# Twenty gate blocks as ten pairs of seven half-depth products

## The chip, the cores and the metric

The kernel runs on one core of one Trainium2 chip. The metric is the device time in microseconds (us) of one execution on that core. The engines are named as the profile names them: PE (TensorE, matmuls), PEld (its weight loads), DVE (VectorE), ACT (ScalarE), POOL (GpSimd) and SP (SyncE, which here only issues DMAs).

## The reference, cut to what matters

One layer of a backbone, for 2048 sample tokens and 128 prompt tokens. The normalized activations go through one wide input projection, three token mixers work on parts of it, and each branch's result is weighted by a sigmoid gate:

```python
proj = jnp.einsum('btd,de->bte', xn, w_in)            # 2176 tokens x 1024 x 7696
qkv, beta, dec, z_a, u_b, v_b, z_b, x_c, z_c, gates = jnp.split(proj, points, axis=-1)
...
br = jnp.stack([o_a, o_b, o_c], axis=2)               # A: gated delta rule, B: spatial MLP, C: Fourier
pb = jnp.einsum('btnw,nwd->btnd', br, w_branch)
gt = jax.nn.sigmoid(gates.reshape(B, T, N_BRANCH, D_MODEL))
merged = jnp.einsum('btnd,btnd->btd', gt, pb)
return jnp.einsum('btd,de->bte', merged, w_out), s_f, s_b
```

The gates are 3072 of the projection's columns: 24 blocks of 128.

## The kernel before

Channels lie on the 128 partitions and tokens run along the free axis. The 2176 x 1024 activations stand in SBUF all along as two float16 halves, `xh` and `xl` (value and remainder), each 128 x 8 x 2176. A weight block of 128 output channels is 128 x 8 x 128, also in two halves (`whi`, `wlo`). A float32-like product is three float16 matmuls per depth step k: whi.xh, whi.xl, wlo.xh; all of them are issued in line 249 (`mm`), so the trace groups them by tile names, not by line. Tokens go in five groups, `TBS`: four of 512 and one of 128; one group of one block is 24 matmuls into one PSUM bank.

A weight block comes by one 512 KB DMA into `wst`, is squared and summed on ACT (L318), gets a scale that is a power of two (DVE, L277 to L279), and is split: `whi` by ACT (L330), `wlo` by DVE (L331: `wst * s - whi`). `getw(n, ahead)` takes the next of one list, `wlist`, and lets so many be prepared ahead; `weight_step()` does one stage of that.

The stages, in order of PE's time in the profiled execution:

- to 160 us: activations, modulation, the first projections
- 160 to 433: q, k, v, 12 blocks, each followed by a conv of three taps over the 2176 tokens (DVE, ACT, POOL) and one store per block
- 433 to about 1010: 22 gate blocks, `gate_block`: per token group 24 matmuls, a sigmoid on ACT (L1496), a store on SP (L1497). Beside them the delta rule's preparation (`kq`, `qr` loads of L999, the triangular inverses of `base_inverse` as a ping-pong between DVE L1126 and POOL L1127, to 870), then the start of the scan. The list's squares of later weights (`later_squares`, ACT) and the sums for the output gate (`gate_rows`: 16 loads of 256 KB, each with four DVE operations of 256 columns, L489 and L491) go beside the gate blocks as well, one step per token group
- 1010 to 1135: branch B's V from four blocks `v4hi`/`v4lo` used together; then U, Z_B and Z_C to 1345, and the Fourier branch C to about 1700
- 881 to about 1600: `scan()`, 34 steps of a chain PE - DVE - ACT - DVE - PE (the tiles `sk`, `sv`, `v`, `u`, `S`; L1316, L1243, L1244, L1338, L1357), beside all of the above
- 1700 to 1732 the last two gate blocks, then `pace.drain()`, and the merges of branches 1 (to 1832) and 2 (to 1980), each 8 blocks of half depth with a multiply by the stored gate (L1821)
- 1980 to 2247: the merge of branch 0 with the output projection, already in seven half-depth products instead of eight (DVE L2003 and L1938 read their banks in between), and the stores.

The order on each engine is fixed when the program is built: a scheduler simulates the program and writes one list per engine; each engine takes its list in order and waits at each instruction for what it needs. What goes beside the gemms is set by `Pace`: a stage calls `pace.tick(us)` with the PE time it has just issued, and the generator (preparation or scan) is taken one step further per quota: `QUOTA` = 1.6 us of gemm per step of the preparation, `SCAN` = 1.15 us per step of the scan. `tc.high_priority()` puts an instruction ahead of others that are ready.

Of the kernel before, what the change touches and what calls it, by code (L numbers as in the profile page):

```python
# [20 lines left out]
P = 128  # L21
D = 1024
KT = 8
# [9 lines left out]
SCAN = 1.15  # L33
# [5 lines left out]
EARLY = 22  # L39
# [157 lines left out]
def hybrid_flow_kernel(ctx: ExitStack, tc: tile.TileContext, x_prompt, x_sample, state_delta, c, c_ctx, w_ada,  # L197
# [178 lines left out]
    for i, (n_, g) in enumerate(_blocks()):  # L376
        wlist.append((w_blk[i], KT, "z" if n_ == C_ZA else "v" if n_ == C_V else "w", 4))
# [3 lines left out]
    goal = [0]  # L381
    wdone, wnext, wread, wlate, bwp, wsteps = [], [0], [], [0], [], []

    def read_next(p_=None):
        if p_ is not None:
            st = sb(p_, [P, D], "ab", bufs=7).rearrange("p (k c) -> p k c", k=KT)
            load(st, wlist[len(wread)][0].rearrange("p (k c) -> p k c", k=KT))
            wread.append(st)
        elif len(wread) < min(len(wdone) - len(wsteps) + 2, len(wlist)):
            src, nkt, tag, bufs = wlist[len(wread)][0:4]  # L390
            wread.append(read_w(src, nkt))

    def begin():

        i = len(wdone)
        if i >= goal[0] or (wlist[i][2] in "bc" and not bwp):
# [426 lines left out]
    vqs = sb(dp, [P, 12], "vqs")  # L823
# [4 lines left out]
    cfs = ExitStack()  # L828
    cf = sb(pool(cfs, "cfp", 1), [P, 2, _CW - _CF], "cf", F16)
    v4s = ExitStack()  # L830
    v4p = pool(v4s, "v4p", 1)
    v4.extend(sb(v4p, [P, 4, KT, P], n_, F16) for n_ in ("v4hi", "v4lo"))
    a1 = ExitStack()
    a1p = pool(a1, "a1p", 2)
    def decays():
# [24 lines left out]
        dtb = sb(a1p, [P, 2, H], "dtb", bufs=1)  # L860
        al = sb(a1p, [P, 2, H], "al", bufs=1)
# [37 lines left out]
        for d in range(2):  # L899
            pt = bank(ps_d, [HN, P])  # L900
            PE.transpose(pt, flat(gam)[:, d * HN:(d + 1) * HN], ident)
            gr = sb(a1p, [HN, P], "gr", bufs=1)
            V.tensor_copy(gr, pt)
            SY.dma_start(gamR[d], gr)
# [38 lines left out]

    flip = [0]
    pace.start(decays(), 1.2)
    for ct in range(12):
        w = getw(1, 2)
        for half in range(1):
# [12 lines left out]
            y = sb(a1p, [P, LP - 2], "cy")  # L961
            V.tensor_scalar(y, raw[:, 0:LP - 2], convw(0, ct), None, ALU.mult)
            V.scalar_tensor_tensor(y, raw[:, 1:LP - 1], convw(1, ct), y, ALU.mult, ALU.add)
            V.scalar_tensor_tensor(y, raw[:, 2:LP], convw(2, ct), y, ALU.mult, ALU.add)
            for c0 in range(0, LP - 2, CQ):
                c1 = min(c0 + CQ, LP - 2)
                A.activation(raw[:, 1 + c0:1 + c1], y[:, c0:c1], AF.Sigmoid)  # L967
                G.tensor_tensor(y[:, c0:c1], y[:, c0:c1], raw[:, 1 + c0:1 + c1], ALU.mult)  # L968
            G.dma_start(qkvD[ct], y)
            if ct < 4 or ct > 7:  # L970
                A.activation(raw[:, 1:LP - 1], y, AF.Square, accum_out=vqs[:, ct:ct + 1])
    pace.drain()
    a1.close()

# [22 lines left out]
    def rows(part, t):  # L997
        x = sb(d2, [P, H, P], "kq" if part else "qr", bufs=3 if part else 2)
# [20 lines left out]
    def prep(g, ci, t, nxt, held):  # L1019
# [21 lines left out]

        more(1, lambda: rows(1, nxt))
        ps = turned(1)
# [29 lines left out]
        for d in range(2):  # L1073
            n_ = sb(d2, [P, WB], "n32", bufs=3)
# [4 lines left out]
            n16 = sb(d2, [P, 2, WB], "n16", F16, bufs=4)  # L1079
# [10 lines left out]
        for d in range(2):  # L1090
            q_ = sb(d2, [P, WB], "n32", bufs=3)
            V.tensor_mul(q_, ps, dc[:, d, :])
            p16 = sb(d2, [P, 2, WB], "n16", F16, bufs=4)
# [306 lines left out]
    def bounds():  # L1400
# [6 lines left out]
        A.activation(sb(dq, [P, 1024], "E"), s0.rearrange("p d x -> p (d x)"), AF.Square, scale=math.sqrt(8.0), accum_out=vqs[:, 4:5])  # L1407
        V.tensor_reduce(bnds[:, 0:1], vqs[:, 0:4], AX.X, ALU.add)
        qs, iqs = scales(bnds[:, 0:1], dp, "qsc")
        yield 1  # L1410
        V.tensor_reduce(bnds[:, 1:2], vqs[:, 8:12], AX.X, ALU.add)
        V.scalar_tensor_tensor(bnds[:, 1:2], bnds[:, 1:2], 8.0 * NTOK, vqs[:, 4:5], ALU.mult, ALU.add)
# [109 lines left out]
    osums = sb(cp, [P, 16], "osums")  # L1522

    def later_squares():


        for i in range(40):
            st = sb(ep, [P, 4, P], "st", bufs=3)
            n, j = (i // KT, i % KT) if i < 24 else (3, i - 24)
            SY.dma_start(st, w_brb[n, j].rearrange("p (k c) -> p k c", k=4) if n < 3 else  # L1530
                         w_outb[j // 2].rearrange("p (k c) -> p k c", k=KT)[:, j % 2 * 4:j % 2 * 4 + 4])
            yield 1
            A.activation(st, st, AF.Square, accum_out=bsums[:, 3 + i:4 + i] if n < 3 else osums[:, j:j + 1])
            yield 1
        b16 = sb(ep, [P, 40], "b16", BF16, bufs=1)
        V.tensor_copy(b16[:, 0:24], bsums[:, 3:27])
        V.tensor_copy(b16[:, 24:40], osums)
        yield 1
        ps = bank(ps_x, [P, 28])
        mm(ps[:, 0:24], ones16, b16[:, 0:24])  # L1540
        halves = b16[:, 24:40].rearrange("p (a j h) -> p a h j", a=2, h=2)
        for i in range(4):
            mm(ps[:, 24:28], ones16, halves[:, i // 2, i % 2], i == 0, i == 3)
        V.tensor_copy(bsums[:, 3:27], ps[:, 0:24])
        exponents(ps[:, 0:24], bscale)
        exponents(ps[:, 24:28], oscale)

    def one_by_one(*gens):
        for gen in gens:
            yield from gen  # L1550
# [222 lines left out]
    def as_pair(hi, lo, src, s):  # L1773
        made = A.activation(hi, src, AF.Copy, scale=s)  # L1774
        V.scalar_tensor_tensor(lo, src, s, hi, ALU.mult, ALU.subtract)  # L1775
        return made

# [19 lines left out]
    pace.drain()  # L1797
    cs_.close()
# [6 lines left out]
    def merge(n, first, inv, step):  # L1805

        for db in range(KT):
# [3 lines left out]
            for t0, tn in TBS:  # L1811
# [6 lines left out]
                ps = bank(ps_d if swap[0] else ps_mm, [P, tn])  # L1818
# [6 lines left out]
                weight_step()  # L1825
# [6 lines left out]
    late_pool = pool(ctx, "late", 1, side="right")  # L1832
# [5 lines left out]
    merge(1, True, inv1, first_step)  # L1838
    cws.extend(getw(KT, 0))
# [342 lines left out]
```

## Time and profile before

| | |
|---|---|
| median of 3 runs | 2252.34 us (2251.59 to 2254.46) |
| the profiled execution | 2248.82 us, span 2247.0 us |
| mean granted TensorE clock | 0.980 |
| busy: PE, DVE, ACT, POOL | 94%, 59%, 47%, 37% of the span |
| matmuls | 16494 |
| DMA traffic | 418.12 MB, mean 186 GB/s |

Read the table as one core that multiplies nearly all the time. "Busy" counts from an instruction's start to its end on its engine; idle time is what the views of waits name. The span is the time from the first to the last instruction; the execution's own time is 1.8 us longer. Line numbers such as L1496 are those of the kernel before, unless the text says "after".

### The profile page before, as it was taken

To read this page: it belongs to the slowest core of one execution; us is meant where nothing else is said; L and a number is where in the kernel's file an instruction comes from. 1 tells how busy PE (TensorE), PEld (TensorE's weight loads), DVE (VectorE), ACT (ScalarE), POOL (GpSimd) and SP (SyncE) were. 2 spreads that over 40 slices of the span, in tenths; PEclk is the share of its full clock that TensorE was granted. 3 is DMA by queue.
4 is the path that set the end of the run, shared out by engine and by line. 5 is a ranking of instruction groups with operands and counts; after the bars stand their busy time and mean duration, and the time that the engine had idled before them with its cause. 6 is when DMAs were issued, how large, how long until landed. Compare 5 with 4: busy or idle time off the path is not lost. (4 is left out here: it accounts for less than half of the span.)

```text
span 2247.0 us, 43529 instructions
## 1 busy us (share of the span) xinstructions
PE 2106.8 (94%) x16494; PEld 1238.3 (55%) x16494; DVE 1321.2 (59%) x2735; ACT 1045.5 (47%) x2404; POOL 841.1 (37%) x1058
## 2 busy tenths in 40 slices
PE   7989999999999999999999999799999996869997
PEld 3454444455555554555656557587775443435553
DVE  5656844356658653457765566667534567346766
ACT  6655743466655553455434555566535231012222
POOL 0221332234524434222333444355221027456654
PEclk9999999999999999999999999899999998989999
DMA  9855731377777854555555565564305985854541
GB/s 383 287 156 173 263 116 61 113 245 244 252 238 228 266 175 134 183 187 155 155 188 164 182 191 164 161 177 142 107 31 185 299 294 183 284 173 141 172 143 47
DMA packets 269170, 418.12 MB, mean 186 GB/s; under 512 B 43400, under 2 KB 142112, under 8 KB 266656
## 3 DMA queue, kind: packets, MB, share of 16 engines
q1 hardware_dynamic: 218240, 328.94, 46.0%
q10 hardware_dynamic: 39824, 44.05, 5.9%
q0 software_dynamic: 10896, 42.36, 5.1%
q8 instruction: 129, 2.11, 0.4%
q14 instruction: 81, 0.66, 0.1%
HBM read 269.79 MB, written 145.45 MB: 185 GB/s over the span
## 5 line engine op out<-in xcount | busy, mean ns | idle before, releaser
L249 PE MATMUL b<-xh,whi 128*128 128x512 f16 (+1 forms) x1920 | 650.0, 348 | 1.9 <-ACT whi L330 1.8
L249 PE MATMUL b<-xl,whi 128*128 128x512 f16 (+1 forms) x1920 | 651.6, 348 | 0.0
L249 PE MATMUL b<-xh,wlo 128*128 128x512 f16 (+1 forms) x1920 | 649.5, 348 | 0.0
L249 PEld LDWEIGHTS <-whi 128*128 128x128 f16 x4416 | 411.7, 98 | 365.5 <-issue 20.5
L249 PEld LDWEIGHTS <-wlo 128*128 128x128 f16 x2208 | 216.6, 98 | 174.1 <-issue 1.1
L249 PEld LDWEIGHTS <-xh 128*128 128x128 f16 x1512 | 119.2, 98 | 29.9
L1127 POOL TENSOR_TENSOR E<-E,XB 128x31 f32<-128x31 f32 (+15 forms) x155 | 97.4, 628 | 95.3 <-DVE XB L1126 88.0
L1496 ACT ACTIVATE sg<-b,winv 128x512 f32<-128x512 f32 (+1 forms) x120 | 74.0, 621 | 125.3 <-PE b L249 97.5
L968 POOL TENSOR_TENSOR cy<-cy,raw 128x545 f32<-128x545 f32 (+1 forms) x48 | 64.5, 1370 | 181.2 <-ACT raw L967 181.2
L249 PEld LDWEIGHTS <-pa 128*128 128x128 f16 x648 | 63.4, 98 | 93.1 <-ACT pa L1774 18.1
L1823 POOL TENSOR_TENSOR mrow<-mrow,sg 128x512 f32<-128x512 f32 (+1 forms) x40 | 46.8, 1177 | 177.7 <-DMA big<-in_w_outb_dram 140.2
L249 PEld LDWEIGHTS <-bhi 128*128 128x128 f16 x640 | 60.9, 99 | 87.7 <-issue 30.2
L249 PE MATMUL b<-xh,bhi 128*128 128x512 f16 (+1 forms) x320 | 86.5, 362 | 22.4 <-DVE sg L1821 20.8
L249 PE MATMUL b<-o,whi 128*128 128x256 f16 (+1 forms) x576 | 93.9, 268 | 14.2 <-DVE gt L1938 12.2
L249 PE MATMUL b<-wlo,xh 128*128 128x128 f16 x544 | 94.6, 219 | 0.0
L249 PE MATMUL b<-whi,xl 128*128 128x128 f16 x544 | 94.6, 219 | 0.0
L249 PE MATMUL b<-whi,xh 128*128 128x128 f16 x544 | 94.6, 219 | 0.0
L1126 DVE TENSOR_TENSOR XB<-XB,E 128x31 f32<-128x31 f32 (+15 forms) x155 | 52.7, 340 | 64.9 <-POOL E L1127 64.7
L331 DVE SCALAR_TENSOR_TENSOR wlo<-wst,wsc,whi 128x1024 f16<-128x1024 f32 x52 | 68.5, 1319 | 36.7 <-ACT whi L330 36.7
L1202 POOL COPY R<-ES 32x256 f16<-32x256 f16 x136 | 55.7, 409 | 91.7 <-PE b L249 86.7
L249 PE MATMUL b<-big,pa 128*128 128x512 f16 x372 | 86.7, 379 | 3.3 <-DVE st L2003 2.4
L249 PE MATMUL b<-xl,pa 128*128 128x512 f16 x276 | 67.0, 387 | 19.1 <-ACT pa L1774 17.8
(537 smaller groups left out, 4508.6 us busy)
## 6 DMA issues: line engine op xcount, KB each, us to landing
wst<-in_w_blk_dram SPq DMA_DIRECT2D x58, 512.0 KB, 3.5
g<-sg SPq DMA_DIRECT2D x96, 256.0 KB, 3.5
sg<-g SPq DMA_DIRECT2D x64, 256.0 KB, 4.4
qkv<-cy POOLq DMA_DIRECT2D x12, 1089.0 KB, 5.3
dc<-dec SPq DMA_DIRECT2D x17, 512.0 KB, 4.3
kq<-qkv SPq DMA_DIRECT2D x34, 256.0 KB, 4.9
kv<-tok POOLq DMA_DIRECT2D x17, 512.0 KB, 4.8
n<-n ACTq DMA_DIRECT2D x34, 256.0 KB, 5.6
```

The costliest lines, as they stand in the source:

```text
L249: newest[0] = PE.matmul(out, l, r, start=start, stop=stop, skip_group_check=reopened)
L331: w.low = V.scalar_tensor_tensor(w.lo, st, s, w.hi, ALU.mult, ALU.subtract)
L968: G.tensor_tensor(y[:, c0:c1], y[:, c0:c1], raw[:, 1 + c0:1 + c1], ALU.mult)
L1126: V.tensor_tensor(t3, X3[:, 0:k, k:k + 1].to_broadcast([P, k, n_]), E3[:, k:k + 1, k:32].to_broadcast([P, k, n_]), ALU.mult)
L1127: G.tensor_tensor(E3[:, 0:k, k:32], E3[:, 0:k, k:32], t3, ALU.subtract)
L1202: G.tensor_copy(R16[32 * B:32 * B + 32, :, :, B], ES[0:32, :, B, :, wR])
L1496: A.activation(sg, ps, AF.Sigmoid, scale=w.inv)
L1823: G.tensor_tensor(mr, mr, gt, ALU.add)
```

## The change

Twenty of the 22 early gate blocks are done two at a time (`two_gates`). With the depth halved (A11, A12: first 1088 tokens; A21, A22: last 1088 tokens; second index: depth half) and the two blocks' weights halved in depth (B11, B21 of one block, B12, B22 of the other), the 2 x 2 product is made with seven half-depth products in the Strassen-Winograd form instead of eight. Each product is 12 matmuls on 368, 360 or 360 tokens (`THIRDS`). Three PSUM banks, R, Y and X, collect them; Y is read, then added into, then read (t2, t3, t4), X once (t1, b22). Between them DVE reads the partial sum out of the bank (`total`, L1673 after).

- The token sums S1 to S4 (`tsum`, in float16 halves) are made beside q, k, v; S1 takes the place of `x[:, 0:4, 1088:]` in `xh`, `xl` (two DMAs from DRAM) while the pairs run, and the original comes back behind them (two more).
- The weights of a pair (`pair_weights`): seven half-depth pairs hi/lo, three subtractions on POOL, in steps set by the product's number (units 1, 8, 10, 11, 15, 17, 19, 20 of 21).
- `later_squares` goes to q, k, v. `gate_rows` goes from the preparation to the last two of the early gate blocks, three steps per token group, just ahead of V.
- The conv of q, k, v goes in four chunks of 545 columns with four stores per block.
- `SCAN` is 1.35; `pace.drain()` stands behind the first merge, which gets `pace.tick`, one `weight_step` fewer per group, and only the `ps_mm` banks while the scan runs.
- Buffers: `kq` 3 to 2, `n32` 3 to 2, `n16` 4 to 3; the pools of `cf` and `v4` are opened behind the pairs.

```diff
-SCAN = 1.15
+SCAN = 1.35
...
-EARLY = 22
+PAIRS = 10
+EARLY = 2 * PAIRS + 2
+HALF = NTOK // 2
+THIRDS = [(0, 368), (368, 360), (728, 360)]
...
+    def token_sums():
+        for l, x in enumerate((xh, xl)):
+            SY.dma_start(a21D[:, l], x[:, 0:4, HALF:])
+        for k in range(4):
+            for a, b, cn in THIRD:
+                f11, f12, f21, f22 = [sb(ep, [P, cn], "sg", bufs=4) for _ in range(4)]
+                for on, f, kk, ts in ((G, f21, k, b), (V, f11, k, a), (G, f22, k + 4, b), (V, f12, k + 4, a)):
+                    on.tensor_tensor(f, xh[:, kk, ts], xl[:, kk, ts], ALU.add)
+                yield 1
+                V.tensor_tensor(f22, f21, f22, ALU.add)
...
+                st = sb(ep, [P, 2, cn], "st", F16, bufs=3)
+                as_pair(st[:, 0], st[:, 1], f22, 1.0)
+                SY.dma_start(s1D[:, :, k, a], st)
+                yield 1
+                for i, f in enumerate((f11, f21, f12)):
+                    as_pair(tsum[:, i, 0, k, a], tsum[:, i, 1, k, a], f, 1.0)
+                    yield 1
...
+            b11, b21, b12, b22 = [st[:, q] for st in sts for q in (slice(0, 4), slice(4, 8))]
+            w0 = slot()
+            self.b11 = put(w0, 0, b11)
+            G.tensor_tensor(b11, b12, b11, ALU.subtract)
+            G.tensor_tensor(t2, b22, b11, ALU.subtract)
+            G.tensor_tensor(b12, b22, b12, ALU.subtract)
+            self.t2 = put(w0, 4, t2)
+            yield 17
...
     pace.drain()
+    for _ in beside:
+        pass
+    first_pair.upto(20)
     a1.close()
+    for l, x in enumerate((xh, xl)):
+        SY.dma_start(x[:, 0:4, HALF:], s1D[:, l])
...
-    gates_rows = one_by_one(later_squares(), gate_rows())
-    for i in range(EARLY):
-        gate_block(2 if i < EARLY - 3 else 4, 2)
...
+        def total(out, ps, other):
+            with tc.high_priority():
+                V.tensor_tensor(out, ps, other, ALU.add)
...
+            R = bank(ps_mm, [P, cn])
+            multiply(R, w.b11, tokens(0, a))
+            p1 = sb(ep, [P, cn], "sg", bufs=4)
+            with tc.high_priority():
+                A.copy(p1, R)
+            Y = bank(ps_mm, [P, cn])
+            multiply(Y, w.t2, s2)
+            u2 = sb(ep, [P, cn], "st", bufs=3)
+            total(u2, Y, p1)
+            multiply(R, w.b21, tokens(4, a), False)
...
+            multiply(Y, w.t3, s3, False)
+            u3 = sb(ep, [P, cn], "st", bufs=3)
+            total(u3, Y, p1)
+            X = bank(ps_mm, [P, cn])
+            multiply(X, w.t1, tokens(0, b))
+            total(u3, X, u3)
+            put_off(u3, d2, b)
+            multiply(Y, w.t4, tokens(4, b), False)
+            total(p1, Y, p1)
+            put_off(p1, d1, b)
+            multiply(X, w.b22, s4, False)
+            total(u2, X, u2)
+            put_off(u2, d2, a)
...
+    for l, x in enumerate((xh, xl)):
+        SY.dma_start(x[:, 0:4, HALF:], a21D[:, l])
+    sums_.close()
...
+    gates_rows = gate_rows()
+    for i in range(2):
+        gate_block(4 - i, 3)
     for _ in gates_rows:
         pass
```

How the lists of the engines change is shown at three places.

DVE in the middle of the preparation, before: beside the ping-pong of the inverses (`XB`, L1126) stand a weight's scale and its `wlo` of 1024 columns.

```order
L328 TENSOR_TENSOR winv_5086<-wsc_5082,xsc_384 128x1
L1126 TENSOR_TENSOR XB_4257<-XB_4257,E_4258 128x192
L331 SCALAR_TENSOR_TENSOR wlo_5007<-wst_4649,wsc_5082,whi_5006 128x1024
L1045 TENSOR_TENSOR tok_5092<-b_5096,ss_624_5093 128x512
L1126 TENSOR_TENSOR XB_4257<-XB_4257,E_4258 128x175
L1126 TENSOR_TENSOR XB_4257<-XB_4257,E_4258 128x156
```

The same place after (L1258 is the former L1126, L947 the `lo` half of `as_pair`, L1673 `total`, L1208 the preparation's `n`):

```order
L1673 TENSOR_TENSOR st_6436<-b_6323,sg_6321 128x360
L1673 TENSOR_TENSOR st_6436<-b_6438,st_6436 128x360
L947 SCALAR_TENSOR_TENSOR wlo_6398<-wst_5888,wsc_6193,whi_6397 128x512
L947 SCALAR_TENSOR_TENSOR wlo_6337<-wt_781_6086,wsc_6193,whi_6336 128x512
L1258 TENSOR_TENSOR XB_6146<-XB_6146,E_6147 128x135
L947 SCALAR_TENSOR_TENSOR wlo_6398<-wst_5889,wsc_6193,whi_6397 128x512
L1673 TENSOR_TENSOR sg_6321<-b_6323,sg_6321 128x360
L1258 TENSOR_TENSOR XB_6146<-XB_6146,E_6147 128x156
L947 SCALAR_TENSOR_TENSOR wlo_6479<-wst_5888,wsc_6193,whi_6478 128x1024
L1258 TENSOR_TENSOR XB_6146<-XB_6146,E_6147 128x175
L1673 TENSOR_TENSOR st_6351<-b_6438,st_6351 128x360
```

The totals, which PE's next product into the same bank waits for, now stand in one queue with the halves of the next pair's weights and with the inverses.

DVE ahead of V, before: the scan's operations and the last of the four `v4lo` (L331).

```order
L1244 SCALAR_TENSOR_TENSOR S_1424_10892<-S_9595,S_1424_10892 128x512
L1197 SCALAR_TENSOR_TENSOR Q_1245_9345<-b_11320,Q_1245_9345 32x256
L277 TENSOR_SCALAR wsc_11370<-b_11368 128x1
L278 TENSOR_SCALAR wsc_11370<-wsc_11370 128x1
L279 TENSOR_SCALAR wsc_11370<-wsc_11370 128x1
L328 TENSOR_TENSOR winv_11374<-wsc_11370,xsc_384 128x1
L1581 COPY vinv_11455<-winv_11374 128x1
L1316 SCALAR_TENSOR_TENSOR sv_10911<-b_10965,neg_1283,sv_10911 128x128 x4
L331 SCALAR_TENSOR_TENSOR v4lo_1315<-wst_11048,wsc_11370,v4hi_1314 128x1024
```

After, ahead of V (L496 is the former L491 of `gate_rows`, L1376 the former L1244, L1489 the former L1357):

```order
L496 SCALAR_TENSOR_TENSOR st_11091<-st_11174,scT_105,st_11091 128x256 x3
L1470 TENSOR_TENSOR sv_11069<-b_11254,beta_1279 128x512
L496 SCALAR_TENSOR_TENSOR st_11091<-st_11174,scT_105,st_11091 128x256
L1363 SCALAR_TENSOR_TENSOR Q_10452<-b_11532,Q_10452 64x256
L496 SCALAR_TENSOR_TENSOR st_11091<-st_11278,scT_105,st_11091 128x256
L1376 SCALAR_TENSOR_TENSOR u_11268<-sv_11069,u_11268 128x512
L496 SCALAR_TENSOR_TENSOR st_11091<-st_11278,scT_105,st_11091 128x256 x2
L1348 SCALAR_TENSOR_TENSOR R_1349_10442<-b_11577,R_1349_10442 64x4x64
L496 SCALAR_TENSOR_TENSOR st_11091<-st_11278,scT_105,st_11091 128x256
L1489 SCALAR_TENSOR_TENSOR S_10807<-S_10807,egl_1281,b_11336 128x128 x4
```

All 64 operations of `gate_rows` now stand among the scan's steps and the four `v4lo`, and each waits for a load of its own.

SP where the gate blocks begin, before: stores of gates (`g`), a weight, the first loads of the preparation.

```order
L1497 DMA g_3908<-sg_3937 128x512
L1497 DMA g_3908<-sg_3996 128x512
L291 DMA wst_4255<-in_w_blk_dram 128x1024
L1497 DMA g_3908<-sg_4088 128x512
L999 DMA kq_3947<-qkv 128x4x128
```

After:

```order
L294 DMA wst_4175<-in_w_blk_dram 128x1024
L1105 DMA xl_97<-s_1315 128x4x1088
L1105 DMA xh_96<-s_1315 128x4x1088
L294 DMA wst_4554<-in_w_blk_dram 128x1024
L1698 DMA g_4512<-sg_4585 128x368
L294 DMA wst_4555<-in_w_blk_dram 128x1024
L1669 DMA g_4512<-st_4610 128x368
L1131 DMA kq_4528<-qkv 128x4x128
```

The two loads of S1 now stand ahead of the first pair's stores, of the second pair's weights and of the preparation's first loads.

More of the change, by code (lines that the diff above doesn't have):

```diff
@@ L944, in hybrid_flow_kernel @@
+    beside = one_by_one(token_sums(), later_squares())
     flip = [0]
@@ L1548, in one_by_one, with part @@
[L1548 to L1554 removed]
+    def part(ps, w, r, fresh):
+        for k in range(4):
+            mm(ps, w[0][:, k, :], r[0][:, k, :], fresh and k == 0, False, not fresh)
+            mm(ps, w[0][:, k, :], r[1][:, k, :], False, False, not fresh)
+            mm(ps, w[1][:, k, :], r[0][:, k, :], False, k == 3, not fresh)
@@ new lines, in hybrid_flow_kernel, with after @@
+    cur = first_pair
+    for i in range(PAIRS):
+        nxt = pair_weights(i + 1) if i < PAIRS - 1 else None
+        def after(u):
+            if nxt is not None:
+                nxt.upto(u)
+            elif u == 15:
+                wlimit[0] += 2
+                fetch(18)
+            elif u > 15:
+                weight_step()
+        two_gates(i, cur, after)
+        cur = nxt
+    for l, x in enumerate((xh, xl)):
+        SY.dma_start(x[:, 0:4, HALF:], a21D[:, l])
+    sums_.close()
```

211 lines of the change are left out of this document (145 added, 66 removed).

## The prediction

> **What bounds the kernel now.** I read the busy shares of the page and the mean clock first, then the table by stage, then who waits for whom inside the stages that change, then single groups for prices.
>
> ```profile
> PE 2106.8 (94%) x16494; PEld 1238.3 (55%) x16494; DVE 1321.2 (59%) x2735; ACT 1045.5 (47%) x2404; POOL 841.1 (37%) x1058
> core 0: 2247.0 us, clock 0.980
> 160.00:440.00 280.00, 280.00 (x1767) 140.06 (x1764) 154.02 (x174) 140.64 (x203) 75.11 (x97) 1.00 0.41 139
> 440.00:881.00 441.00, 434.21 (x2758) 236.85 (x2756) 267.26 (x676) 245.99 (x685) 180.35 (x266) 1.00 0.71 223
> 881.00:1016.00 135.00, 131.32 (x1178) 77.33 (x1176) 60.05 (x160) 62.18 (x138) 37.72 (x65) 0.99 0.62 193
> 1345.00:1600.00 255.00, 231.19 (x3262) 192.76 (x3260) 168.63 (x423) 159.18 (x473) 114.52 (x157) 0.95 0.52 156
> ```
>
> The columns of the last four rows are window, length, then busy time (instructions) of PE, PEld, DVE, ACT, POOL, the granted clock, the DMA share and GB/s. PE is the bound: 94% of the span, and in the stages that the change touches first (q, k, v and the gate blocks) it multiplies without a gap at full clock. So a matmul column taken out of 440 to 1016 us is time, as long as nothing else becomes late. DVE has 174 us free of 441 there. The Fourier stage is the exception, with 24 us of PE idle and a clock of 0.95.
>
> **The columns.** The last gate block stands alone, so its matmul times are clean: it starts at 1710.07 and its last matmul is followed by the next stage's first at 1732.13.
>
> ```profile
> 1710.07 0.38 PE L249 MATMUL b<-xh,whi 128*128 128x512 f16 x1
> ...
> 1730.79 0.22 PE L249 MATMUL b<-xh,whi 128*128 128x128 f16 x1
> ...
> 1732.13 0.17 PE L249 MATMUL b<-bsc2b,ones 128*128 128x1 bf16 x1
> ```
>
> 96 matmuls of 512 columns take 1730.79 - 1710.07 = 20.72, or 0.2158 us each; 24 of 128 take 1.34, or 0.0558 each. The line through both is 0.4167 ns per column and 2.4 ns per matmul, so 368 columns cost 0.1557 and 360 cost 0.1524 us. A block is 22.06 us, two are 44.12. A pair is 7 products of 12 matmuls for each third: 7 x 12 x (0.1557 + 2 x 0.1524) = 38.68 us. That is 5.44 less per pair, **-54.4 us** for ten. (Twelve matmuls more per pair are counted in it.) Nothing else on PE changes in amount.
>
> **Pairs: the reopened banks.** PE writes Y, DVE adds it into a partial sum, and only then may PE add the next product into Y. There are 3 reopenings per third: T3 and T4 into Y, b22 into X; b21 into R waits likewise for ACT's copy. I count 90 for DVE. Between a bank's last matmul and its reopening lies at least one product of 12 matmuls, 1.83 us. DVE's part:
>
> ```profile
> L2003 DVE TENSOR_TENSOR st<-b,sg x16: 676/681/692, 2003.3 to 2224.6; 128x512 f32<-128x512 f32 x16
> L1938 DVE SCALAR_TENSOR_TENSOR gt<-b,binv,gt x72: 342/475/485, 1917.6 to 2195.8; 128x256 f32<-128x256 f32 x64, 128x128 f32<-128x128 f32 x8
> PE b L249 <- DVE gt L1938: 5.1, 6, 2.2
> PE b L249 <- DVE st L2003: 2.4, 4, 1.5
> 2085.00:2100.00 15.00, 11.70 (x78) 7.44 (x77) 12.55 (x15) 4.67 (x6) 8.23 (x7) 1.00 0.61 211
> ```
>
> Between 0.475 us at 256 and 0.681 at 512 columns, a total of 360 is about 0.56 us, which fits into 1.83 when DVE is free. The output projection at the end is made in the same way and is the nearest measure: 24 reopenings with a slack of 12 x 0.216 = 2.6 us cost 2.4 us of PE waits for L2003 (the first two rows are duration min/median/max; the third and fourth are total us, times, longest). The lower end for ninety is nothing, or -6.8 if even the present idle of that stage went; the upper takes both waits, (2.4 + 5.1)/24 x 90 = 28 us. I take L2003 alone, 0.1 us each: **+9**.
>
> What makes them late is DVE's load in that stage, since the queue is in order:
>
> ```profile
> L331 DVE SCALAR_TENSOR_TENSOR wlo<-wst,wsc,whi x52: 1272/1284/2135, 127.5 to 1660.2; 128x1024 f16<-128x1024 f32 x52
> L1095 DVE SCALAR_TENSOR_TENSOR n<-n,n 128x512 f16<-128x512 f32 x34 | 23.9, 709 | 1.8 <-ACT n L1094 1.6
> L491 DVE SCALAR_TENSOR_TENSOR st<-st,scT,st x56: 466/479/924, 134.7 to 732.6; 128x256 f32<-128x256 f32 x56
> L489 DVE TENSOR_SCALAR st<-st,scT x8: 331/334/351, 134.2 to 715.8; 128x256 f32<-128x256 f32 x8
> L1126 DVE TENSOR_TENSOR XB<-XB,E x155: 177/359/426, 481.3 to 869.8; 128x31 f32<-128x31 f32 x10, 128x60 f32<-128x60 f32 x10, 128x87 f32<-128x87 f32 x10, 128x112 f32<-128x112 f32 x10
> DVE XB L1126 <- POOL E L1127: 64.7, 99, 2.4
> L1823 POOL TENSOR_TENSOR mrow<-mrow,sg 128x512 f32<-128x512 f32 (+1 forms) x40 | 46.8, 1177 | 177.7 <-DMA big<-in_w_outb_dram 140.2
> L1243 ACT ACTIVATE v<-sv 128x512 f16<-128x512 f32 x12 | 7.5, 624 | 3.0 <-DVE sv L1316 3.0
> ```
>
> Added: 150 totals x 0.56 = 84; the `lo` halves, 46 of 512 columns x 0.71 and 10 of 1024 x 1.28, instead of 20 x 1.28, +20. Gone: the part of `gate_rows` that ran there, about 24. So 267 + 84 + 20 - 24 = 347 us of some 440, 79% instead of 61%. The preparation's inverses end at 870, only 11 us ahead of the scan; but they are paced with room, and DVE already waits 64.7 us for POOL in that ping-pong, out of which the added queue can come. POOL gets 27 subtractions at the 1.18 us of L1823, 32 us; ACT gets fewer squares and more copies, about 0.62 us each as in L1243. Both stay below 60%.
>
> [...]
>
> **The swap of S1, the first weights, q, k, v.** Two loads of 1.09 MB go out right behind the last q, k, v matmul and are first needed by T1, the fifth product.
>
> ```profile
> gt<-g SPq DMA_DIRECT2D x8, 1024.0 KB, 5.5
> xt<-in_x_t_dram SPq DMA_DIRECT2D x3, 2048.0 KB, 11.2
> ```
>
> 2.2 MB at 2 MB in 11.2 us land after about 12 us; four products are 4 x 1.868 = 7.5 us, and the preparation's first matmuls can stand between. The bounds are 0 and 4; **+2**. Behind the loads on SP wait the next weights (not needed for 38 us) and the first `kq` (the preparation has its slack). The way back is shorter than one gate block's first two token groups, 8 us of 22; for that and the block's own weight **+1** (0 to 3). In q, k, v, DVE gets 12 units of 10 operations of 360 columns, 67 us, and the first pair's halves, 9: 154 + 76 = 230 of 280. ACT gets 48 copies and 40 squares at L1243's 0.62, 55: 196 of 280. POOL gets 24 sums and 36 more stores; even at 1.18 us for each, 71, it stands at 146. The copies that free PE's banks are put first, so all of it is covered by 280 us of gapless PE; if the cover fails, a late `wlo` costs PE a few us. I take **+1** (0 to 6).
>
> **The start of V.** This is where I expect the largest give-back. `gate_rows`, 56 x 0.479 + 8 x 0.334 = 29.5 us of DVE, lay in the slack of the preparation and now lies in the last two gate blocks, where the scan and the four weights of V (4 x 1.28) want DVE too. Counted over the list with these durations, from the second block's weight to the last `v4lo` DVE has 67 us of work where PE has 61. `gate_rows` works on two free buffers, and each load has to land before two to four of these operations:
>
> ```profile
> st<-in_w_ada_dram SPq DMA_DIRECT2D x16, 256.0 KB, 3.7
> L1316 DVE SCALAR_TENSOR_TENSOR sv<-b,neg,sv 128x128 f32<-128x128 f32 x48 | 13.5, 344 | 2.5 <-PE b L249 2.4
> L1244 DVE SCALAR_TENSOR_TENSOR v<-sv,v 128x512 f16<-128x512 f32 x12 | 11.5, 960 | 1.2 <-ACT v L1243 1.2
> ```
>
> A hop of the scan is 4 x 0.344 + 0.624 (L1243 above) + 0.96 = 3.0 us, and in the new list three of its steps stand there nearly back to back, with 0.5 to 2 us of matmuls between a hop's ends: about 5 us short per step. The two shortages overlap; 67 - 61 = 6 is the least that I see, 6 + 15 = 21 both in full. Bounds 0 (the loads' waits fall into gaps) and 25; I take 12, and 2 for the clock that falls after such idling (below): **+14**.
>
> **The Fourier stage.**
>
> ```profile
> PE b L249 <- DMA ES<-ei: 7.0, 4, 3.8
> PE b L249 <- ACT o L1253: 4.5, 5, 2.0
> PE b L249 <- DVE u L1244: 3.0, 3, 1.5
> 1400.00:1410.00 10.00, 6.26 (x95) 5.73 (x93) 4.89 (x10) 4.58 (x14) 3.46 (x6) 0.89 0.63 175
> 1410.00:1420.00 10.00, 8.00 (x77) 6.19 (x75) 7.64 (x24) 7.20 (x22) 4.65 (x5) 0.50 0.51 144
> 1418.65 0.63 PE L249 MATMUL b<-xl,whi 128*128 128x512 f16 x1
> ```
>
> 12 of the scan's steps run there. PE idles 23.8 us, and the clock of 0.95 costs 231 x 0.05 = 11.6 more: the rows show it at half after a slice with 3.7 us of idling (the same matmul takes 0.63 us instead of 0.38). At 1.35 the steps stand further apart. Summing over the list what each hop has too little, 10.7 us before become 3.7. That is -7 and, at 11.6/23.8 of clock per idle us, -3.4; the scan's last steps go to the last group and the first merge, +1: **-9**. Bounds: -20, where the waits for the scan go altogether, and +5, where they come back at the later place. With one weight step fewer and half the banks in merge 1: **+2** (-2 to 8).
>
> **Sum** on the profiled execution: 2248.8 - 54.4 + 9 + 2 + 1 + 1 + 14 - 9 + 2 = 2214.4. The profiled execution lies 3.5 below the median of the runs (2252.34), so the forecast is **2218 us**. A difference under 0.2%, 4.5 us, can't be told from no change.
>
> **The rivals.**
>
> 1. The totals bind. If the 90 reopenings come late by 0.48 us on average, the 9 us become 43 and nothing is left: (2252.3 - 2218 + 9)/90. At 0.6 us each it ends at 2218 - 9 + 54 = 2263, slower. For it: DVE at 79%, and single operations of 1.3 us (`lo` of 1024) that may stand in front of a total. Against it: 0.1 us each in the row of L2003, with DVE at 12.55 of 15 us in the slice at 2085, and the totals have priority. 6%.
> 2. The clock falls in the pairs. Every short wait of PE at a reopening could bring the clock down, as in 1410 to 1420. If the pairs' 387 us ran at 0.90, 387 x 0.11 = 43 more: 2261. Against it: the slice at 2085 idles 3.3 of 15 us in such waits and keeps 1.00. [...] 3%.
> 3. Most of it stays: V starts without waiting (0), the pairs lose 3, the Fourier stage gives 15: 2218 - 14 - 6 - 6 = 2192. For it: in 881 to 1016 DVE is busy only 60 of 135 us, so the added 29.5 may find room. 22%.
> 4. The give-backs are larger: V's start 25, the Fourier stage +2, the pairs 15: 2218 + 11 + 11 + 6 = 2246. 9%.
>
> My own sum, with its terms between 2200 and 2236, has the remaining 60%. The range that holds 8 in 10 leaves out rivals 1 and 2 and the far ends of 3 and 4: 2190 to 2244. Faster: 60 + 22 + 6 of the last, 88%; the same 4%; slower 8%.
>
> **What would show it.** In the pairs' stage: length of ten pairs 387 us plus the preparation's own matmuls, so about 54 less to the same point; waits of PE for L1673 of 5 to 15 us in all, clock 1.00, DVE near 79%. Ahead of V: PE waiting for `v4lo`, L496 or the scan, 8 to 20 us in a stretch of 60. In the Fourier stage: idle down from 24 to about 17, clock above 0.95. Wrong it would be if L1673 led the list of PE's releasers with over 40 us, if q, k, v stretched beyond 280, or if the merges grew by what the scan leaves them.

## The result, and the profile after

The changed kernel takes 2290.03 us (median of 4 runs, 2282.67 to 2294.62) where the kernel before took 2251.97: a ratio of 1.0167, with an interval of 1.0136 to 1.0197. It is slower by 38 us, where I had forecast 34 us faster. The profiled execution took 2294.62 us, the slowest of the four, so what the stages below add up to is 46 us and not 38.

The first line of the changed kernel's page:

```profile
PE 2082.5 (91%) x16604; PEld 1281.9 (56%) x16604; DVE 1542.1 (67%) x3103; ACT 1122.8 (49%) x2595; POOL 959.5 (42%) x1158
```

Its span with the mean granted clock:

```profile
core 0: 2292.8 us, clock 0.963
```

Its table by stage (columns as before: window, length, busy time and instructions of PE, PEld, DVE, ACT, POOL, then the clock, DMA share, GB/s):

```profile
153.00:464.00 311.00, 269.98 (x1450) 130.47 (x1446) 244.02 (x385) 189.36 (x362) 121.55 (x145) 0.94 0.48 160
464.00:964.00 500.00, 455.91 (x3217) 303.78 (x3215) 375.92 (x787) 304.71 (x807) 247.20 (x311) 0.98 0.64 206
964.00:1058.00 94.00, 73.52 (x565) 42.55 (x564) 61.43 (x164) 35.85 (x71) 30.12 (x41) 0.84 0.75 230
```

PE has less to do and is less busy: 91% instead of 94%. The rows are q, k, v, the ten pairs, and the two gate blocks ahead of V. In all three PE now has gaps and a lower clock; before, the first had none.

To set the stages of both kernels against each other I counted each stage's matmuls, times their spacing at full clock (0.216 us for 512 columns, 0.1557 for 368, 0.056 for 128 and so on): the content. What a stage takes beyond that is its loss, idle time and slow clock together.

| stage | before: length, loss | after: length, loss | change of the loss |
|---|---|---|---|
| start, q, k, v | 427.3, 37.0 | 463.8, 73.3 | +36.3 |
| twenty gate blocks, ten pairs | 523.5, 12.9 | 499.5, 59.4 | +46.5 |
| two gate blocks, to V | 59.3, 1.2 | 94.3, 32.6 | +31.4 |
| V, U, Z | 356.0, 4.6 | 341.3, -0.1 | -4.7 |
| Fourier | 321.8, 39.9 | 319.0, 27.2 | -12.7 |
| last two gate blocks, merge 1 | 136.5, 3.8 | 159.5, 15.3 | +11.5 |
| merges 2 and 0, output | 422.5, 89.6 | 415.5, 82.5 | -7.1 |

The content falls by 55.3 us (2058.1 to 2002.8), the losses grow by 101.2, and 46 is the difference of the spans. The saving is there to a microsecond; the first three rows take 114 us back, twice as much.

The first row hides two changes of opposite sign. The first matmul of q, k, v comes at 153.1 us instead of 166.6, so the start became 13.5 us shorter; q, k, v itself takes 310.7 us instead of 260.7 and loses 50 where it lost nothing. The shorter start goes with the squares of later weights on ACT: in the kernel before, they ran from 19 to 134 us, long before the gate blocks beside which they stand in the text; in the changed kernel they run from 326 to 389 us.

**q, k, v.** Two slices of 20 us of the same table:

```profile
240.00:260.00 20.00, 17.72 (x102) 8.71 (x100) 19.28 (x27) 8.93 (x12) 3.20 (x2) 1.00 0.78 246
260.00:280.00 20.00, 0.00 (x0) 0.00 (x0) 18.54 (x28) 14.20 (x21) 7.26 (x9) 0.54 0.66 238
```

And the row of PE's timeline that ends the gap (in brackets the idle time before it and what ended it):

```profile
284.39 0.58 PE L252 MATMUL b<-xh,whi 128*128 128x512 f16 x1 [26.50 <-ACT raw L1082]
```

PE stands still for 26.5 us while DVE is busy 93 to 96% of the time in these slices. The wait is put down to ACT's copy into `raw`; there are two `raw` tiles, and the copy can only be made when the conv of the block before last has let go of its tile. That conv is queued on DVE behind decays and token sums.

**The pairs.** PE's waits from 464 to 945 us (total, times, longest):

```profile
PE b L252 <- DVE st L1673: 19.0, 13, 4.2
PE b L252 <- ACT sg L1697: 5.3, 3, 2.4
PE b L252 <- DVE wlo L947: 4.3, 2, 3.3
PE b L252 <- DVE sg L1673: 4.0, 5, 1.1
```

The totals (L1673, into `st` and `sg`) lead, as feared, though with 23 us, 25.5 to the stage's end, and not 43. What stood ahead of a late one is seen in DVE's timeline (start, duration):

```profile
670.82 1.41 DVE L1258 TENSOR_TENSOR XB<-XB,E 128x175 f32<-128x175 f32 x1
672.87 1.37 DVE L1258 TENSOR_TENSOR XB<-XB,E 128x156 f32<-128x156 f32 x1 [0.64 <-POOL E L1259]
674.15 1.23 DVE L1167 TENSOR_SCALAR ss<-ss 128x4 f32<-128x4 f32 x1
675.29 0.52 DVE L1673 TENSOR_TENSOR st<-b,sg 128x360 f32<-128x360 f32 x1
```

and in POOL's at the same place:

```profile
670.38 1.65 POOL L1048 TENSOR_TENSOR wst<-wst,wst 128x512 f32<-128x512 f32 x1 [0.63 <-DVE wlo L947]
672.31 0.53 POOL L1259 TENSOR_TENSOR E<-E,XB 128x175 f32<-128x175 f32 x1 [0.28 <-DVE XB L1258]
672.79 1.26 POOL L1049 TENSOR_TENSOR wt<-wst,wst 128x512 f32<-128x512 f32 x1
674.01 1.34 POOL L1050 TENSOR_TENSOR wst<-wst 128x512 f32<-128x512 f32 x1
```

The inverses' step of 0.37 us takes 1.4, and an operation on 128 x 4 numbers, 0.165 in the median, takes 1.23. Each begins or runs while POOL subtracts two weight halves, and ends within 0.2 us of that subtraction's end.

**Ahead of V.** PE's timeline after its last gate matmul at 1017 us, cut to the waits:

```profile
1028.82 1.33 PE L252 MATMUL b<-v,R 128*128 128x128 f16 x11 [2.68 <-DVE v L1376]
...
1048.24 0.27 PE L252 MATMUL b<-u,kn 128*128 128x128 f16 x1 [2.75 <-ACT u L1375]
...
1051.95 1.01 PE L252 MATMUL b<-st,sel 128*2 128x256 f32 x2
1052.89 0.18 PE L252 MATMUL b<-wscb,ones 128*128 128x1 bf16 x1
...
1057.57 0.81 PE L252 MATMUL b<-v4hi,xh 128*128 128x512 f16 x3
```

For 40 us PE does the bare chain of the scan, with a wait at every hop. V can't start: the sum of its last weight (`wscb,ones`, at 1052.89) stands in PE's list behind two steps of the scan and the first half of the last sum of `gate_rows` (`st,sel`). DVE had its operand ready 32 us earlier:

```profile
1020.10 0.16 DVE L266 CAST wscb<-wss 128x1 bf16<-128x1 f32 x1 [1.28 <-ACT v4lo L321]
```

The product at 1021.82 is the third weight's; from the last weight's own product to V's first matmul it is 4.7 us.

### The profile page after: what moved, and what is told of

The parts are those of the page before. It is cut to its first block, busy times and chain, and to the rows that moved or that the text cites. A ratio compares the mean times of both kernels' runs of the same rounds, so it can differ in the third digit from the quotient of the medians.

```text
span 2292.8 us, 44609 instructions
## 1 busy us (share of the span) xinstructions
PE 2082.5 (91%) x16604; PEld 1281.9 (56%) x16604; DVE 1542.1 (67%) x3103; ACT 1122.8 (49%) x2595; POOL 959.5 (42%) x1158
## 3 DMA queue, kind: packets, MB, share of 16 engines
q1 hardware_dynamic: 227552, 337.85, 46.5%
## 5 line engine op out<-in xcount | busy, mean ns | idle before, releaser
L252 PEld LDWEIGHTS <-whi 128*128 128x128 f16 x4496 | 426.2, 99 | 380.4 <-issue 101.7
L252 PE MATMUL b<-xh,whi 128*128 128x512 f16 (+3 forms) x1600 | 536.9, 342 | 62.8 <-ACT raw L1082 37.1
L252 PE MATMUL b<-xl,whi 128*128 128x512 f16 (+3 forms) x1600 | 537.5, 342 | 0.0
L252 PE MATMUL b<-xh,wlo 128*128 128x512 f16 (+3 forms) x1600 | 536.4, 342 | 1.0 <-DVE wlo L947 1.0
L252 PEld LDWEIGHTS <-wlo 128*128 128x128 f16 x2248 | 223.1, 99 | 165.0 <-issue 8.4
L252 PE MATMUL b<-tsum,whi 128*128 128x360 f16 (+1 forms) x720 | 168.6, 320 | 9.8 <-DVE sg L1673 4.0
L252 PE MATMUL b<-tsum,wlo 128*128 128x360 f16 (+1 forms) x360 | 115.0, 319 | 3.3 <-DVE wlo L947 3.3
L252 PE MATMUL b<-big,bhi 128*128 128x512 f16 (+1 forms) x320 | 82.7, 351 | 4.7 <-DVE o L1528 2.8
L1258 DVE TENSOR_TENSOR XB<-XB,E 128x31 f32<-128x31 f32 (+15 forms) x155 | 62.0, 400 | 37.0 <-POOL E L1259 36.4
L252 PEld LDWEIGHTS <-xl 128*128 128x128 f16 x824 | 74.4, 98 | 16.0 <-issue 0.7
```

Of the source, the lines that this page charges most:

```text
L252: newest[0] = PE.matmul(out, l, r, start=start, stop=stop, skip_group_check=reopened)
L1258: V.tensor_tensor(t3, X3[:, 0:k, k:k + 1].to_broadcast([P, k, n_]), E3[:, k:k + 1, k:32].to_broadcast([P, k, n_]), ALU.mult)
```

## The experiments

Each kernel is the changed one with the edit shown, or the one with three edits where the text says so. Times are medians; "to the first pair" is from the start to the first product of a pair, 427.3 us to the same place before and 463.8 after. Losses and the time to the first pair are those of one profiled execution. Where an edit doesn't touch them they differ all the same: the pairs' loss is 55 to 61 in five kernels with the same pairs, and to the first pair it is 460.8 to 463.8 in four kernels with the same q, k, v and 461.7 to 467.5 in four with the squares first.

**`gate_rows` beside the last two gate blocks.**

```diff
-            acc = sb(ep, [P, 512], "st", bufs=3).rearrange("p (g c) -> p g c", g=2)
+            acc = sb(sp, [P, 512], "gacc").rearrange("p (g c) -> p g c", g=2)
...
-    gates_rows = gate_rows()
+    gates_rows = iter(())
...
-    gates_rows = own
+    gates_rows = both(own, gate_rows())
```

> The changed kernel with gate_rows taken out of the two gate blocks ahead of V and put beside the last two gate blocks ahead of the merges, with three buffers of its own. Theory A (gate_rows' 16 loads and its place in the PSUM ring that the weights' scales share hold V's last weights back while PE has nothing but the scan): the stretch from the pairs' end to V falls from 94 us to 60 to 68, the whole to about 2262. Rival B (two blocks are too short for V's four weights, which before were prepared beside three, and three scan steps stand back to back): the stretch stays above 80, the whole above 2278. Rival C: it falls, but 4 MB of loads and 64 DVE operations ahead of the merges cost the same there: whole about 2285.

2264.65 us, ratio to before 1.0051 (1.0034 to 1.0068): 25 us less. The row of the two gate blocks:

```profile
961.00:1015.00 54.00, 51.65 (x406) 28.24 (x405) 19.70 (x56) 26.44 (x50) 18.28 (x30) 1.00 0.72 227
```

and the largest of PE's waits there:

```profile
PE b L252 <- ACT v4hi L333: 1.6, 1, 1.6
```

94 us have become 54, and the loss 3 instead of 33. Theory A holds: the two blocks are long enough for V's weights, and the scan's steps get in between. The edit takes away the loads, DVE's work and the sums on PE together; that it was the place on PE is read from the trace above. The 64 operations cost 6 us ahead of the merges and in merge 1 (losses of 8.6 and 12.3 instead of 5.2 and 10.1).

**The subtractions on DVE.**

```diff
-            G.tensor_tensor(b11, b12, b11, ALU.subtract)
+            V.tensor_tensor(b11, b12, b11, ALU.subtract)
...
```

and so for the other three of a pair.

> The changed kernel with the four subtractions of each pair's weights on DVE instead of POOL (40 operations of 512 columns, some 0.68 us each, 27 us more on DVE). Theory A (POOL holds DVE: in the pairs 31 DVE operations were longer than usual by 30 us in all and ended with one of these subtractions, and totals stood behind them): the loss of PE in the pairs, 59 us (idle and slow clock), falls to 40 to 48, the whole to about 2277. Rival B (DVE's load itself makes the totals late, at 376 of 500 us, and 27 more make it worse): the loss grows to 62 to 75, the whole to about 2297.

2272.65 us, 1.0087 (1.0057 to 1.0117): 17 us less, with 40 more operations on DVE. The pairs' loss is 47.5 instead of 59.4. The inverses' step, first of the changed kernel, then of this one (duration min/median/max):

```profile
L1258 DVE TENSOR_TENSOR XB<-XB,E x155: 181/368/1715, 520.3 to 955.3; 128x31 f32<-128x31 f32 x10, 128x60 f32<-128x60 f32 x10, 128x87 f32<-128x87 f32 x10, 128x112 f32<-128x112 f32 x10
```

```profile
L1258 DVE TENSOR_TENSOR XB<-XB,E x155: 177/358/427, 515.9 to 941.1; 128x31 f32<-128x31 f32 x10, 128x60 f32<-128x60 f32 x10, 128x87 f32<-128x87 f32 x10, 128x112 f32<-128x112 f32 x10
```

The pairs' row of this kernel:

```profile
461.00:949.00 488.00, 453.23 (x3213) 302.57 (x3213) 366.46 (x828) 303.97 (x808) 195.41 (x271) 0.99 0.65 211
```

The long ones are gone. DVE is busy 366 us instead of 376, although it does 27 us more: by 376 + 27 - 366 the holds were worth an estimated 37. Theory A holds, rival B does not; but it is 12 of the 46 us. (The rest lies in stages that the edit does not touch, the Fourier stage above all.)

**Both, with the squares ahead of the token sums.** The third edit turns `one_by_one(token_sums(), later_squares())` round; alone:

> The changed kernel with one line turned: beside q, k, v the squares of later weights go first and the token sums behind them. In the changed kernel q, k, v took 310.7 us instead of 260.7, with DVE at 95 to 100% from 200 to 300 us, where the generator of decays runs too. Theory A (the token sums fall on the same 100 us as the decays; conv falls behind, the two raw buffers are not free and PE waits): q, k, v falls to 265 to 280 us and the whole to about 2255. Rival B (the conv in four chunks, its 48 stores and its longer chain between the engines cost the time wherever the sums stand): q, k, v stays above 300, the whole within 8 us of 2290. Rival C (what DVE is short of over the whole stage, 230 us by my count and 38 us more of holds by POOL): q, k, v stays at 290 to 300, only later in the stage.

2284.08 us, 1.0146 (1.0106 to 1.0185); to the first pair 461.7. A miss that told nothing on A, since the sums did not move away from the decays: the first remainder of a sum ran at 155.8 us in the changed kernel and at 165.1 here. The squares went to 19 us, where they had been before the change, and the start is as long again as before (165.3 us); q, k, v takes 296 instead of 311 us, and the two cancel. The scheduler takes what is ready, not what stands first in the text. The three edits together:

> The three edits together: token sums behind the squares, gate_rows beside the last two gate blocks, subtractions on DVE. If each removes its own loss and they don't meet (theories A): 35 + 28 + 13 us off 2290, about 2214. Rival: what is released early meets the next bound (weights, the scan's chain, the merges), and 25 us or more of it come back: 2240 or above.

2246.92 us, 0.9973 (0.9956 to 0.9990): 43 us less than the changed kernel, just ahead of the one before, and in the rival's range, because the first 35 us are still there (462.6 to the first pair).

**The sums really late.** Squares first, and each sum's additions ordered behind the newest conv:

```diff
+                with tc.issue_after(conv_last[0].ins), tc.issue_after(conv_last[1].ins):
+                    for on, f, kk, ts in ((G, f21, k, b), (V, f11, k, a), (G, f22, k + 4, b), (V, f12, k + 4, a)):
...
```

> The changed kernel with the squares first and the first additions of each token sum ordered on DVE and POOL behind the newest conv operation of the text, so that the sums begin behind the fifth block's conv (turning the two generators alone left them where they were: the scheduler put them at 160 us all the same, and from the start to the first pair it took 461.7 us instead of 463.8). From the start to the first pair: before 427.3. Theory A (sums and decays collide in the same 100 us): 435 to 445 us, the whole about 2268. Rival C (DVE is full over the whole stage: 154 us before, sums 64, the conv in four chunks 18 more, holds by POOL 28 more, of 270): it only shifts, 455 to 465, the whole within 8 us of 2288.

2297.47 us, 1.0192 (1.0150 to 1.0233); to the first pair 467.4. The 26 us wait is gone, and the time is lost later, at the stage's end, where DVE is at 100% from 360 to 380 and from 420 to 440:

```profile
PE b L252 <- ACT whi L946: 12.3, 1, 12.3
PE b L252 <- ACT raw L1084: 10.8, 9, 2.5
PE b L252 <- DVE wsc L280: 7.6, 1, 7.6
```

Now the first pair's weights are late. That is rival C, with both numbers some 2 us beyond its range. With the other two edits:

> Three edits together: the sums ordered behind the conv of the fifth block, gate_rows beside the last two gate blocks, the pairs' subtractions on DVE. With the earlier version of the first edit the three gave 2247. By theory A of the sums 20 us less, about 2227; by rival C no change, 2240 to 2250.

2258.88 us, 1.0019 (0.9999 to 1.0039), 469.2 to the first pair: worse than with the sums early, as rival C has it and by more than it said.

**No token sums.** `tsum` and S1 are constants.

> The changed kernel without the token sums: the halves S1 to S4 are set to a constant by six memsets on POOL, so the gates are not the reference's; all products, loads and stores remain. Theory A and C (the sums, 64 us of DVE, 24 operations of POOL and their holds, are what q, k, v loses): from the start to the first pair 427 to 434 us, the whole about 2257. Rival B (conv in chunks, 48 stores, squares on ACT, the first pair's weights): it stays above 445, the whole above 2272.

2260.66 us, 1.0035 (1.0012 to 1.0058); to the first pair 437.6, a little above the first range. The stage's row:

```profile
168.00:438.00 270.00, 265.38 (x1456) 129.54 (x1454) 181.78 (x266) 141.39 (x234) 112.06 (x131) 0.99 0.41 145
```

26 of the 36 us are the sums. The squares have moved to 19 us here too; beside the kernel with only the squares first (461.7 us) the sums are worth 24. The loss that is left, 8 us in q, k, v itself, is the rest of the stage's changes. Without them DVE has 182 us of work, with them 244.

**The first tap on ACT**, on top of the three edits.

```diff
-                V.tensor_scalar(y, raw[:, c0:c1], convw(0, ct), None, ALU.mult)
+                A.activation(y, raw[:, c0:c1], AF.Copy, scale=convw(0, ct))
```

> The kernel of the three edits (squares first, gate_rows late, subtractions on DVE; 2247 us) with the first tap of the conv, 48 multiplications of 545 columns, on ACT instead of DVE: some 24 us less on DVE in q, k, v, 26 us more on ACT, which had 200 of 300 us. If DVE's sum of work sets the length of q, k, v (theory C: shifting the sums later only moved the wait to the stage's end, leaving them out took 26 us off), from the start to the first pair falls from 462.6 to 440 to 450 and the whole to 2225 to 2235. Rival D (the waits stand in ACT's queue, where the copies that free PE's banks and the conv's sigmoids are): no change or longer, 460 to 475, the whole 2245 or above.

2243.79 us, 0.9961 (0.9943 to 0.9980), the lowest median of all; to the first pair 457.4 instead of 462.6, between the two ranges. Some 5 us for 24 us of DVE, no more than the spread of that time: theory C is right in direction at most, not in size.

**The sums spread** from the third block to the tenth, on top of that.

> The kernel of the three edits with the first tap on ACT (2244 us), and the token sums spread: two steps per token group, from the third block's conv to the tenth block, each ordered on DVE and POOL behind the newest conv operation; the squares run in the first twelve groups. Sums at 160 us met the decays (first pair at 462), sums behind the fifth block met the first pair's weights (467), and the tap on ACT alone left DVE above 90% from 180 to 340 us and below 60% from 360 (457). If it is DVE's load in each stretch that holds PE, spread evenly it fits: start to first pair 436 to 447 us, the whole 2222 to 2233. If the stage is short of DVE time altogether, or the chain of a conv behind each sum sets the pace: 452 to 465, the whole 2238 to 2250.

2247.57 us, 0.9982 (0.9965 to 0.9999); to the first pair 460.8, the second range. PE's waits from 168 us to the first pair:

```profile
PE b L252 <- ACT raw L1084: 14.4, 16, 3.4
PE b L252 <- ACT whi L946: 9.5, 1, 9.5
```

No long wait is left inside the blocks, but sixteen short ones, and again the first pair's weights at the end. DVE is down to 8 of 20 us there (420 to 460), so it is no longer DVE's load: ACT, which takes its list in order, does the conv's steps a block late, each waiting some 1.8 us for DVE or 0.7 for POOL, with the copies that free PE's banks and the `whi` behind them. That is read from ACT's timeline only; whether a shorter conv chain would end it wasn't tried.

**No reopened banks**: Y collects t2, t3, t4 and X t1, b22, with three totals at the end; the partial sums between them are left out.

> The changed kernel without the three partial sums per third that are read out of a bank between two products: Y collects t2, t3 and t4 in one run, X t1 and b22, and three totals are read at the end (the gates of the pairs are not the reference's; PE's products are the same, DVE does 90 instead of 150 totals, 32 us less). In the changed kernel PE lost 59 us in the pairs, 25.5 of them in waits for the totals. Theory A (the reopened banks are the loss, since PE must wait for a busy DVE there): the loss falls to 20 to 32 us, the whole to about 2258. Rival B (DVE and ACT are late with everything in that stage, and the weights and the preparation take the waits over): the loss stays above 42, the whole above 2274.

2297.93 us, 1.0191 (1.0157 to 1.0225); the pairs' loss 52.3 instead of 59.4. (The whole is no shorter, because the two blocks ahead of V lose 9 us more.) Rival B, and the finding against my own rival 1: with no read between the products PE still waits for the totals, fewer of them, and for other things that DVE and ACT are late with.

```profile
PE b L252 <- DVE st L1673: 13.3, 8, 3.8
PE b L252 <- ACT T L1194: 6.3, 3, 4.1
PE b L252 <- DVE wlo L947: 4.5, 2, 3.5
PE b L1193 <- DVE tok L1177: 4.4, 5, 1.6
```

**The lower halves on ACT**, on top of the three edits: `as_pair` in `put` becomes two copies on ACT, so the lower half is a second copy of the value and not the remainder.

> The kernel of the three edits (2247 us) with the lower halves of the pairs' weights written by ACT as a second copy of the value instead of by DVE as the remainder: 60 operations, some 45 us, go from DVE to ACT in the pairs' stage (the gates of the pairs are not the reference's, since the lower half is not the remainder). PE loses 46 us there now. With 90 of the totals gone the loss had fallen by 7 only. Theory E (DVE's whole queue is too full, 366 of 487 us, and whatever stands in it comes late): the loss falls to 20 to 32. Rival F (the chain through ACT and DVE is long whoever does it, ACT at 320 of 487 gets as late): the loss stays at 42 to 60.

2244.29 us, 0.9968 (0.9949 to 0.9987); the pairs' loss 29.9 instead of 46.0. The pairs' row:

```profile
466.00:936.00 470.00, 447.18 (x3219) 301.83 (x3217) 319.34 (x761) 337.29 (x861) 182.65 (x271) 1.00 0.68 216
```

and PE's largest waits from 464 to 945 us (L1674 is `total` here):

```profile
PE b L252 <- DVE st L1674: 6.2, 11, 1.3
PE b L252 <- ACT sg L1698: 4.9, 5, 2.3
```

Theory E: 42 us off DVE (361 in the kernel of the three edits) give PE 16, and the waits for totals into `st` fall to a third (from 19.0 there; with those into `sg` from 19.6 to 9.1), with ACT now the busier of the two. So most of it comes from what stands in DVE's queue, not from the reads between the products. The amount of DVE's work alone is not the measure: the kernel without reopened banks has 35 us less on DVE as well (341 of 492) and gained 7. Which operations count is not separated: here long ones went, of 0.75 to 1.3 us, and with them a step of the weights' own chain. Of the 16 us the whole shows 3; the two blocks ahead of V lose 10 instead of 3, and the rest is spread over other stages.

**The scan's pace back at 1.15**, on top of the three edits.

> The kernel of the three edits (2247 us) with the scan's pace back at 1.15 us of matmuls per step. If the pace of 1.35 brought the gain in the Fourier stage (loss of 23 us there against 40 before the change), the loss goes back to 35 to 45 and some 8 us come back behind it, where the scan's end runs beside the last gate blocks and the first merge (losses of 7 and 8): whole 2250 to 2260. Rival: the stage's waits have other causes (loads, ACT), the loss stays at 20 to 27 and the whole falls to 2238 to 2244.

2265.14 us, 1.0066 (1.0041 to 1.0091). Slower by 18 us, more than expected, and for other reasons: the Fourier stage loses 25.1 instead of 23.1; the two blocks ahead of V lose 9.4 instead of 2.9, and merge 1 15.9 instead of 8.3. The pace of 1.35 is worth those 18 us, but only 2 of it in the Fourier stage.

## Why the prediction was wrong, step by step

- **The columns, -54.4: right.** The count gives -55.3.
- **q, k, v, +1 (0 to 6): measured +50 in the stage itself, +36 with the start, which became shorter. This step failed.** (The swap of S1, +2, cost nothing to be seen: PE never waited for its loads; what was late at the first pair were its weights, 7 us.) I divided DVE's work by the length of the stage, 230 of 280 us, and called it covered. My sum was low: the conv in four chunks takes 0.50 + 0.78 + 0.78 us four times per block, 8.3 us, against 6.3 in three long operations (1.36 + 2.49 + 2.49), 24 us in all, and the changed kernel shows 244. In it DVE's operations also ran beyond their usual length, by 38 us against 10 before, which I put down to POOL; no run here takes POOL's work out of that stage. Above all the mean hid the place: before, DVE was already busy for 81 of the 100 us from 200 to 300, with the decays, and the sums went there, because the scheduler puts ready work early. The condition that I wrote down, "if q, k, v stretched beyond 280", came true. Leaving the sums out takes 24 to 26 us back; that it was only their place is not shown, since later sums cost as much.
- **The pairs, +9 (-6.8 to 28): measured +46.5. Failed.** The term was priced from the waits of a stage with 24 reopenings, as if the reads were the cost. Without those reads most of the loss stays; 42 us of work taken off DVE return 16. DVE's load was forecast well, 79% against 75% measured; what failed is the step from that load to the wait. What I called the cover of the totals, DVE's idle time of 93 us, was no cover here, where PE waits for so many operations of one queue in order. The rival with the totals was near in size of the loss (43 against 46.5), by luck: the waits for totals are 25.5 of the stage's 59.4.
- **What POOL's subtractions do to DVE had no term in the sum, and cost a quarter of the pairs' loss.** I counted 27 subtractions, three per pair as the list of the change has it; there are four per pair, 40. I took DVE's operations at their medians, L331 at 1.284 us with its longest at 2.135. In the changed kernel 150 totals, which read PSUM and SBUF, never took more than 0.561 us, and the 136 of L1208, also out of PSUM, never more than 0.351, while a `wlo` of 512 columns went from 0.75 to 2.97 and XB from 0.37 to 1.72. With the subtractions on DVE the longest `wlo`, those of 1024 columns counted in, takes 1.35 and the longest XB 0.43. Moving them gave 12 of the pairs' 46 us.
- **V's start, +14 and +1 for the block (0 to 25): measured +31.4. Failed by size.** Place and culprit were right, `gate_rows` ahead of V; the size and the mechanism were not. I priced DVE's shortage and the scan's hops, 6 to 21 us; what held V was the order on PE, the last weight's sum 32 us behind its operand. With `gate_rows` elsewhere the loss is 3.
- **Fourier, -9: measured -12.7; the reason was mostly another.** With the old pace, in the kernel of the three edits, the stage still loses 25 instead of 40. What else made it better stays open.
- **Merges, +2: measured +4.4** with the last gate blocks (11.5 less 7.1). V, U and Z, at nothing in the sum, gave 4.7 back; why stays open.

## What to carry to other kernels

When work is moved into a stage, add it to the engine's load in the 50 us where the scheduler will put it, not to the stage's mean: here 230 of 280 us was a full queue from 200 to 280 us, with DVE busy 93 to 100% of it in slices of 20 us. A saving on the bounding engine is only as good as the slack of the engine that has to feed it; seven products for eight bring 5.4 us per pair, and cost 4.7 in their stage and 3.6 ahead of it, where DVE is busy 75% (376 of 500 us) and 78% (244 of 311) of the time. Before pricing a new wait, ask what takes DVE's time behind its back: here a step of DVE of 0.165 us in the median took 1.23 us beside a POOL subtraction of 1.34.

## What the runs showed of the hardware that I had not expected

A DVE operation on 128 x 4 numbers in SBUF, `ss` (L1167), 0.165 us in the median, took 1.23 us beside a POOL subtraction of 128 x 512 that took 1.34, and ended 0.03 us after it; four of its 34 took 1.23 to 1.25 us in this way. So here the hold was as long for a tiny operation, one that reads a single tile; with the subtractions on DVE its longest is 0.67. The hold reads as busy time, not as waiting: the changed kernel's DVE shows 376 us of 500, and moving 40 operations onto it brought that down to 366 of 488. And after 26.5 us of standing still PE's matmuls of 512 columns took 0.63 us until 288.6 and 0.38 from 288.9 on, some 4.5 us after the restart at 284.39 (mean clock 0.51 from there to 288.9, 1.00 from 288.9 to 295). The ten started until 288.6 lie 0.42 us apart instead of 0.22, an estimated 2 us that came on top of the wait's own length.
